# Identity fills between two phases: twelve copies moved from VectorE to GpSimd, behind a zero fill that now comes first

## The chip, the cores and the metric

The kernel runs on one core of one Trainium2 chip. A core has five engines that run their own queues of instructions and meet through semaphores: TensorE (PE in the profile, with its weight loads as PEld), VectorE (DVE), ScalarE (ACT), GpSimd (POOL) and SyncE (SP), whose queue issues the DMAs. The metric is the device time of one execution in microseconds (us); lower is better.

## The reference

One layer of a bidirectional mixer. 128 context tokens and 2048 latent tokens of width 1024 are normalised, modulated and projected; half the channels (8 heads of 64) go through an RWKV-7 recurrence in both directions, the other half through a gated short convolution, and both through one output projection.

```python
def step(S, inp):                       # per direction and head, S is 64 x 64
    r_t, w_t, k_t, v_t, kk_t, a_t = inp
    s_kk = einsum('bdhij,bdhj->bdhi', S, kk_t)
    S = S * w_t[..., None, :] - s_kk[..., :, None] * (kk_t * a_t)[..., None, :] \
        + v_t[..., :, None] * k_t[..., None, :]
    return S, einsum('bdhij,bdhj->bdhi', S, r_t)
...
y = ys[:, 0] + flip(ys[:, 1])           # both directions
y = groupnorm(y) * gn_w + gn_b + bonus * v
ya = y * silu(g_a)
yb = b_gate * short_conv(c_gate * u_conv) * silu(g_b)
out = x + gate * (concat(ya, yb) @ w_out)      # then a last RMS norm
```

Outputs are the new context and latent tokens and the final context states.

## The kernel before

The program has three phases. Phase 1 projects blocks of 384 tokens on TensorE with fp32 split in two halves (lines 182 to 184), prepares the recurrence's operands and spills them to device memory. Phase 2 runs the recurrence in chunks of 64 tokens: 17 stages, each with eight units in either direction. Phase 3 is the output projection and the last norm.

In phase 2 the recurrence within a chunk becomes linear algebra. For each stage the kernel forms masked products of the chunk's operands (`Gm`, `Fm`, evicted by VectorE at L1037 and by ScalarE at L1048 and L1051), inverts the 16 triangular 64x64 systems of the stage, and builds one 128x128 operator E for each unit, which then carries the state from chunk to chunk (L1220, L1246). The inverse goes through these steps, with the names used in the profile:

- VectorE gathers the diagonal blocks in `dg` (L1058), turns them into `ab` (L1063) and does a first elimination step (L1081, then L1082, which writes `ab` again). ScalarE begins the result `zt` (L1073 to L1075; L1075 reads `ab`).
- GpSimd runs the elimination in 15 rounds of three operations, `ztmp` (L1091) and twice `zt` (L1094).
- VectorE turns `zt` into `zr` and `zd` (L1102, L1105). ScalarE copies the diagonal parts from `zd` into the tile `zb` (L1111). TensorE and ScalarE fill the off-diagonal part: psU (L1119), copied at L1122, psW (L1127), evicted into `zb` at L1130.
- TensorE multiplies `zb` with F (psX, L1171); ScalarE writes the result into the stack `stf` (L1175).
- The operators are products of two stacks (psE, L1189), masked by VectorE (L1194).

A stack is a tile of 128 partitions by two blocks by 2 x 8 x 64 values, 8 KB a partition. `stf0` and `stf1` hold one factor for the two directions, `stg0` and `stg1` the other one in even stages, `sth0` and `sth1` in odd ones. In partitions 0 to 63 block 0 of every stack is eight identities beside each other, for each of two heads; that part is written once, by `presetS`. The other parts are filled in every stage by DMA (L956) and by ScalarE (L1160, L1161, L1175). `zb` is zeroed once by `zero` (L907) and keeps its zero quarter for all stages.

All of these tiles are made in `setup_rest`, which runs at the start of phase 2's main part, when phase 1 has given back its memory. The pools are stacks: `stf`, `stg`, `zb` and the small `zr`, `zd` lie in the pool `l1` one behind the other, over the memory of phase 1's activations (two tiles of 24 KB on that side). `sth` lies in a pool on the other side. A tile's first write waits for the last users of the phase 1 tiles under it.

The order of the queues: in the main part of phase 2 and in phase 3, TensorE, VectorE and ScalarE follow an order that is written out in the source (`SEQ`, `LATE`). GpSimd, the DMA queue and everything between the phases, `setup_rest` and the work of the first stages ahead of the written order, are ordered by the framework's planner, which lets each engine take what its model of the program says is ready. In a queue, an instruction that waits holds all behind it.

```python
i2b = lambda n: B.I2[:].unsqueeze(1).broadcast_to((128, n, 64))
...
SEQ: "... bu+1 Ev010 I+2 S20 ... ab+3 ... pre+3 ... zr+2 ... zd+2 ..."   # word+d: of the stage d ahead
```

The words I, ab, pre, zr are the steps above: in the body of stage s the inverse of stage s+2 starts and the `ab` of stage s+3 is made.

Of the kernel before, what the change touches and what calls it, by code (L numbers as in the profile page):

```python
# [6 lines left out]
F32 = mybir.dt.float32  # L7
# [808 lines left out]
def phase2(K):  # L816
    nc, tc, A, S = K.nc, K.tc, K.A, K.S
    V, G, P, T = nc.vector, nc.gpsimd, nc.scalar, nc.tensor
    D = nc.sync.dma_start
    MF, MG, ME = (0, 1), (0, 1), (2, 3)  # L820
    B = Ctx()
    O = Ctx()
# [27 lines left out]
    def new_slot(pool):  # L850
        i = len(B.slots)
        B.slots.append([tuple(pool.tile([128, 8, w], F32, tag=f"{n}{i}{d}", name=f"{n}{i}{d}", bufs=1) for n, w in (("F", 128), ("GA", 128), ("Q", 64))) for d in range(2)])
# [8 lines left out]
    def setup_rest():  # L861
        O.l0 = Pool(K, "p2l0", "left")
        O.l1 = Pool(K, "p2l1", "left")
        O.pS = Pool(K, "p2S", "left", 4, PSUM)
        O.p2 = Pool(K, "p2s", "left", 2, PSUM)
        O.r2 = Pool(K, "p2r2", "right")
        new_slot(O.r2)
        cp = O.l0
        vec = cp.tile([128, 4], F32, name="vec2")
        D(vec[:], A["vec"][:, V_GW:V_GW + 4])  # L870
        B.gwh = cp.tile([128, 4], F32, name="gwh")
        V.tensor_scalar(B.gwh[:], vec[:], 0.5, None, ALU.mult)
        B.geps = cp.tile([128, 1], F32, name="geps")
        V.memset(B.geps[:], 64e-5)
        B.pc = cp.tile([64, 2, 8, 34], F32, name="pc")
        for d in range(2):
            D(B.pc[:, d], S[f"pc{d}"].rearrange("(e c) n -> c e n", c=64))

        B.fs = ring(O.l1, 2, [128, 2, 2, 8, 64], "stf", presetS)
        B.gs = ring(O.l1, 2, [128, 2, 2, 8, 64], "stg", presetS)  # L880
        B.gs2 = ring(O.r2, 2, [128, 2, 2, 8, 64], "sth", presetS)
        B.zb = O.l1.tile([128, 16, 64], F32, name="zb")
        zero(B.zb)

    def ring(pool, n, shape, name, init=None):
        l = [pool.tile(shape, F32, name=f"{name}{i}") for i in range(n)]
        if init:
            for t_ in l:
                init(t_)

        def get():
            l.append(l.pop(0))
            return l[-1]
        get.tiles = l
        return get
# [10 lines left out]
    def zero(t_):  # L906
        G.memset(t_[:], 0.0)  # L907
# [5 lines left out]

    def presetS(t_):
        for hd in range(2):
            V.tensor_copy(t_[0:64, 0, hd], B.I2[0:64].unsqueeze(1).broadcast_to((64, 8, 64)))

    def tl(shape, tag, b, pool=None, dt=F32):
        return (pool or O.l0).tile(shape, dt, tag=tag, name=f"{tag}_{K.u()}", bufs=b)
# [465 lines left out]

    def main():
        setup_rest()
        for b, n, t in order_of(range(-3, 0)):
            K.body = b
# [259 lines left out]
```

## Time and profile before

| | |
|---|---|
| median of 3 runs | 1586.96 us (1585.86 to 1587.49) |
| profiled execution, its time | 1585.76 us |
| its span, first to last instruction | 1583.9 us |
| mean granted TensorE clock | 0.982 |
| TensorE busy | 1501.7 us, 95% |
| VectorE busy | 1137.6 us, 72% |
| ScalarE busy | 770.6 us, 49% |
| GpSimd busy | 570.9 us, 36% |
| chain of waits by engine | PE 57%, POOL 18%, DVE 10%, issue 7%, DMA 5%, ACT 3% |

How to read it. Busy time is a share of the whole span, over stages with different limits; the chain of waits follows the work that ended last back from the end. In the chain, a line gives the start, the length and what ran. In a timeline of one engine a line gives the start, the time, the engine, source line and operation, output and input tiles with their shapes, the count of instructions merged into the line, and in brackets the idle time before it with what ended it. In a list of waits the numbers are the total, the times and the longest. In a list of stretches come the length, busy time and count of instructions of TensorE, its weight loads, VectorE, ScalarE and GpSimd, then the granted TensorE clock, the DMA engines' busy share and GB/s. In a list of groups, the busy time and the mean in ns of one stand behind the count.

The last projection of phase 1 ends near 948.8 us; the scan of phase 2 runs from there to about 1340 us, with parts of phase 3 mixed in towards its end.

### The profile page before, as it was taken

The page shows a single profiled execution, that of the slowest core. Times are in us where ns is not written, and L with a number is a line of the kernel's source. Part 1 is how long each engine was busy: PE and PEld are TensorE (multiplying, and loading weights), DVE is VectorE, ACT ScalarE, POOL GpSimd, SP SyncE. Part 2 cuts the span into 40 slices and gives each one's busy share as a digit, 9 for nine tenths or more (in the row PEclk, how much of TensorE's full clock was granted, in tenths as well). Part 3 has the DMA queues.
Part 4 walks back from the last instruction along what each step waited for, and adds up shares of the span by engine and source line. Part 5 has one row for each costly group of instructions (what it writes and reads, how often), then busy time and mean ns, then how long its engine had stood idle before and what let it go on. Part 6 is the DMA issues. An engine that isn't in the chain of part 4 may idle for free.

```text
span 1583.9 us, 39394 instructions
## 1 busy us (share of the span) xinstructions
PE 1501.7 (95%) x16208; PEld 1382.2 (87%) x16208; DVE 1137.6 (72%) x1960; ACT 770.6 (49%) x1460; POOL 570.9 (36%) x961
## 2 busy tenths in 40 slices
PE   5899999999999999999999998999999887899998
PEld 2799999999999999899999997888888776778786
DVE  5889996673999735349985438899898977746533
ACT  4466652432555213225551117887778767523221
POOL 0033331000333100013322705888888885212221
PEclk8899999999999999999999998999999999999999
DMA  9569999663878865447897537567576754645442
GB/s 371 197 168 269 269 268 335 216 222 112 218 231 227 203 230 181 145 137 209 262 242 271 184 125 193 151 177 195 167 205 167 186 149 149 186 134 188 147 144 93
DMA packets 204580, 313.78 MB, mean 198 GB/s; under 512 B 58089, under 2 KB 147561, under 8 KB 190321
## 3 DMA queue, kind: packets, MB, share of 16 engines
q1 hardware_dynamic: 168816, 311.13, 63.3%
q10 hardware_dynamic: 35584, 0.14, 1.4%
q8 instruction: 127, 2.08, 0.6%
q14 instruction: 53, 0.43, 0.1%
HBM read 208.05 MB, written 103.17 MB: 196 GB/s over the span
## 4 chain that ended last, share of the span: by engine, by line
PE 57%; POOL 18%; DVE 10%; issue 7%; DMA 5%; ACT 3%; SPq 1%; ACTq 0%; DVEq 0%; POOLq 0%
POOL zt L1094 11%; POOL ztmp L1091 7%; PE psu L1503 4%; PE psu L1505 4%; PE psu L1504 4%; PE mmb L182 2%; PE mmb L184 2%; PE mmb L183 2%; PE mmc L182 2%; PE mmc L184 2%; PE mmc L183 2%; PE mmu L184 2%; PE mmu L182 2%; PE mmgb L183 2%; PE mmgb L182 2%
## 5 line engine op out<-in xcount | busy, mean ns | idle before, releaser
L1094 POOL TENSOR_TENSOR zt<-zt,ztmp 128x30 f32<-128x30 f32 (+7 forms) x510 | 217.5, 426 | 39.8
L1091 POOL TENSOR_TENSOR ztmp<-ab,zt 128x60 f32<-128x60 f32 (+7 forms) x255 | 137.7, 540 | 65.3 <-DVE ab L1082 45.6
L410 POOL TENSOR_TENSOR sh<-rawl 128x384 f32<-128x384 f32 (+1 forms) x48 | 47.1, 997 | 210.4 <-ACT rawl L401 210.4
L1220 PEld LDWEIGHTS psS<-sv,E 128*64 128x64 f32 x2176 | 81.5, 137 | 40.7 <-DVE sv L1246 18.7
L1220 PE MATMUL psS<-sv,E 128*64 128x64 f32 x2176 | 102.4, 228 | 15.1 <-DVE sv L1246 10.4
L1194 DVE TENSOR_TENSOR E<-psE,msk 128x512 f32<-128x512 f32 x136 | 90.6, 682 | 20.7 <-PE psE L1189 19.8
L1568 POOL TENSOR_TENSOR z<-z,x 128x512 f32<-128x512 f32 x32 | 42.7, 1337 | 148.9 <-DVE z L1562 86.2
L1175 ACT ACTIVATE stf<-psX 64x512 f32<-64x512 f32 x136 | 80.3, 591 | 10.6 <-PE psX L1171 8.1
L434 POOL TENSOR_TENSOR hsl<-sq,hsh 128x384 fp32r<-128x384 f32 (+1 forms) x24 | 32.5, 1356 | 141.9 <-ACT hsh L429 141.9
L1246 DVE TENSOR_TENSOR sv<-psS,pc 64x128 f32<-64x128 f32 x254 | 62.3, 271 | 20.0 <-PE psS L1220 19.4
L182 PE MATMUL mmg<-h,w 128*128 128x384 f32 (+1 forms) x216 | 70.9, 328 | 0.0
L183 PE MATMUL mmg<-h,w 128*128 128x384 f32 (+1 forms) x216 | 70.8, 328 | 0.0
L184 PE MATMUL mmg<-h,w 128*128 128x384 f32 (+1 forms) x216 | 70.7, 327 | 0.0
L219 POOL TENSOR_TENSOR hslq<-ssq,hshq 128x384 fp32r<-128x384 f32 (+1 forms) x4 | 4.8, 1207 | 174.8 <-ACT hshq L218 110.3
L182 PE MATMUL mmv<-h,w 128*128 128x384 f32 (+1 forms) x192 | 63.9, 333 | 3.7 <-ACT lf L665 3.1
L182 PE MATMUL mmb<-h,w 128*128 128x384 f32 (+1 forms) x192 | 63.6, 331 | 3.8 <-DMA w<-scr_wsp 3.8
L184 PE MATMUL mmb<-h,w 128*128 128x384 f32 (+1 forms) x192 | 63.6, 331 | 0.0
L183 PE MATMUL mmb<-h,w 128*128 128x384 f32 (+1 forms) x192 | 63.3, 330 | 0.0
L184 PE MATMUL mmv<-h,w 128*128 128x384 f32 (+1 forms) x192 | 63.3, 330 | 0.0
L183 PE MATMUL mmv<-h,w 128*128 128x384 f32 (+1 forms) x192 | 63.2, 329 | 0.0
L182 PE MATMUL mmc<-h,w 128*128 128x384 f32 (+1 forms) x192 | 63.1, 329 | 0.0
L184 PE MATMUL mmc<-h,w 128*128 128x384 f32 (+1 forms) x192 | 62.9, 327 | 0.1
(311 smaller groups left out, 5018.2 us busy)
## 6 DMA issues: line engine op xcount, KB each, us to landing
w<-scr_wsp SPq DMA_DIRECT2D x68, 1024.0 KB, 6.5
scr_wsp<-w SPq DMA_DIRECT2D x34, 1024.0 KB, 6.4
rr<-scr_ops SPq DMA_DIRECT2D x32, 1024.0 KB, 6.4
scr_ops<-xs SPq DMA_DIRECT2D x160, 192.0 KB, 6.5
wr<-in_win SPq DMA_DIRECT2D x34, 512.0 KB, 6.6
x<-in_x SPq DMA_DIRECT2D x17, 512.0 KB, 3.8
wadas<-in_wada SPq DMA_DIRECT2D x8, 1024.0 KB, 13.9
sv<-scr_vt SPq DMA_DIRECT2D x32, 256.0 KB, 4.0
```

The source lines that it names most:

```text
L182: T.matmul(ps[:, :n], w[:, 0, k], hh[:, 0, k, :n], start=k == 0, stop=False)
L183: T.matmul(ps[:, :n], w[:, 0, k], hh[:, 1, k, :n], start=False, stop=False)
L184: T.matmul(ps[:, :n], w[:, 1, k], hh[:, 0, k, :n], start=False, stop=k == 7)
L1091: G.tensor_tensor(tv, ab[:, j:j + 2, j + 2:32].unsqueeze(1).broadcast_to((128, kn, 2, n)), zt[:, :kn, j:j + 2].unsqueeze(3).broadcast_to(( ...
L1094: G.tensor_tensor(zt[:, :kn, j + 2:32], zt[:, :kn, j + 2:32], tv[:, :, r], ALU.subtract)
L1175: P.activation(g.fs[64:128, :, hd, e::2], g.ps["X"][e][hr_].rearrange("p a (b t) -> p b a t", b=2), AF.Copy, scale=-1.0)
L1194: V.tensor_tensor(g.E[n][:, k:k + 2].rearrange("p a b c -> p (a b) c"), pe[:].rearrange("p a b c -> p (a b) c"), B.msk[:, ME[g.d]].unsquee ...
L1220: T.matmul(g.sp[i // 4][r, q, hd, :], g.E[n][:, k, hd, r], g.sv[:, u, hd, :], start=True, stop=True)
L1246: V.tensor_tensor(dst, g.sp[i // 4][0:64, q], B.pc[0:64, d, 2 * p:2 * p + 2, c:c + 1].broadcast_to((64, 2, 64)), ALU.mult)
L1503: T.matmul(ps[:], mh[:, n], hi[:, cs], start=start and n == 0, stop=False)
L1504: T.matmul(ps[:], mh[:, n], lo[:, cs], start=False, stop=False)
L1505: T.matmul(ps[:], ml[:, n], hi[:, cs], start=False, stop=stop and n == 3)
```

## The change

`zb` is allocated and zeroed ahead of the three rings of stacks, and the identities are copied by GpSimd (`G`) in place of VectorE (`V`). There are three rings of two stacks with two copies each: twelve copies of 64 x 512 values. `zb` thereby lies in front of the stacks in its pool and no longer behind them.

```diff
             D(B.pc[:, d], S[f"pc{d}"].rearrange("(e c) n -> c e n", c=64))
 
+        B.zb = O.l1.tile([128, 16, 64], F32, name="zb")
+        zero(B.zb)
         B.fs = ring(O.l1, 2, [128, 2, 2, 8, 64], "stf", presetS)
         B.gs = ring(O.l1, 2, [128, 2, 2, 8, 64], "stg", presetS)
         B.gs2 = ring(O.r2, 2, [128, 2, 2, 8, 64], "sth", presetS)
-        B.zb = O.l1.tile([128, 16, 64], F32, name="zb")
-        zero(B.zb)
...
     def presetS(t_):
         for hd in range(2):
-            V.tensor_copy(t_[0:64, 0, hd], B.I2[0:64].unsqueeze(1).broadcast_to((64, 8, 64)))
+            G.tensor_copy(t_[0:64, 0, hd], B.I2[0:64].unsqueeze(1).broadcast_to((64, 8, 64)))
```

## The prediction

> **What bounds the kernel now.** First the page's chain of waits, by line:
>
> ```profile
> POOL zt L1094 11%; POOL ztmp L1091 7%; PE psu L1503 4%; PE psu L1505 4%; PE psu L1504 4%; PE mmb L182 2%; PE mmb L184 2%; PE mmb L183 2%; PE mmc L182 2%; PE mmc L184 2%; PE mmc L183 2%; PE mmu L184 2%; PE mmu L182 2%; PE mmgb L183 2%; PE mmgb L182 2%
> ```
>
> GpSimd's inverse (L1091, L1094) is the costliest single thing on it. Next, who released GpSimd between 945 and 1345 us, how busy it is in one stage of the scan, and where its unbroken run ends:
>
> ```profile
> POOL ztmp L1091 <- DVE ab L1082: 16.5, 2, 14.5
> ...
> 964.00:988.00 24.00, 23.13 (x591) 20.39 (x584) 16.59 (x31) 16.88 (x33) 20.24 (x44) 0.95 0.61 170
> ...
> 1306.52 0.31 POOL L1091 TENSOR_TENSOR ztmp<-ab,zt 128x60 f32<-128x60 f32 x1
> ```
>
> GpSimd waited for VectorE's `ab` twice: 14.5 us before the first inverse of the scan, and once more for 2.0 at the very end (16.5 less 14.5). In between, inverses stand one behind the other, 20.24 of 24 us busy, the rest issue. Whatever moves the start of that first inverse therefore moves the whole scan. So I read the chain between the phases, on which the edit lies:
>
> ```profile
> 948.86 0.42 DVE bsv L590
> ...
> 950.04 1.07 DVE stf L916 x3
> 951.12 0.67 DVE stg L916 x2
> 951.78 0.40 DVE ov L619
> 952.18 0.67 DVE stg L916 x2
> 952.86 0.96 DVE zr L1102
> ...
> 953.96 1.23 PE psU L1119 x39
> 955.20 0.67 DVE sth L916 x2
> 955.87 2.39 DVE GA L1037 x4
> ...
> 959.91 2.08 DVE ab L1063
> 961.99 0.28 DVE F L1037
> 962.27 1.02 DVE dg L1081
> ...
> 963.48 0.76 DVE ab L1082
> ...
> 964.37 0.30 POOL ztmp L1091
> ```
>
> From the last projection to GpSimd's start, 948.86 to 964.37, the chain is VectorE almost alone, and the twelve copies of L916 stand in it. That is the part the change takes out.
>
> **The change, part by part.**
>
> *VectorE loses 12 copies.* From the end of `bsv` (949.28) to the first `stg` (951.12) is 1.84; `stg` twice 0.67; and the four `sth`:
>
> ```profile
> 954.49 1.38 DVE L916 COPY sth<-I 64x512 f32<-64x512 f32 x4
> ...
> 948.76 1.98 PE L1019 MATMUL psGm<-rr 64*64 64x128 f32 x64
> ```
>
> Together 1.84 + 1.34 + 1.38 = 4.55 us. `GA` could then start at 951.3; its products (psGm) are out at 950.74, so TensorE does not hold it. VectorE alone would give 4.55.
>
> *But ScalarE runs beside it, nearly without a gap*, and VectorE's next steps need it:
>
> ```profile
> 948.86 0.62 ACT L1160 COPY stg<-GA 64x512 f32<-64x512 f32 x1 [2.49 <-PE mmb L184]
> ...
> 952.72 0.61 ACT L1161 COPY stg<-Q 64x512 f32<-64x512 f32 x1
> 953.85 0.63 ACT L1073 ACTIVATE zt<-idt 128x512 f32<-128x512 f32 x1 [0.52 <-DVE gwh L872]
> ...
> 954.65 2.51 ACT L1111 COPY zb<-zd 32x512 f32<-32x512 f32 x4
> 957.19 0.62 ACT L1160 COPY sth<-GA 64x512 f32<-64x512 f32 x1
> ...
> 959.49 1.18 ACT L1122 COPY zd<-psU 32x512 f32<-32x512 f32 x2
> 960.70 0.65 ACT L1051 COPY F<-psFm 128x256 f32<-128x256 f32 x2
> 962.02 0.42 ACT L1075 ACTIVATE zt<-ab,ph 128x16 f32<-128x16 f32 x1 [0.68 <-DVE ab L1063]
> ```
>
> The brackets are all its idle time from 948.86 on: 0.52 (it waited for VectorE's first `zr`, now early) and 0.68 (for `ab`). If the planner keeps ScalarE's order, the copies of F (L1051) can start only 0.52 earlier, 960.18, and the first of the pair is out at about 960.50 (half of 0.65). VectorE's mask of F, which comes between the two `ab` steps and needs that copy, then starts about 960.55 where the chain has 961.99: 1.4 us earlier. The second copy ends at 960.83 and L1075 at 961.25, both ahead of the last `ab` step (963.48 less 1.4 = 962.1), so they add nothing. Of the 4.55 us, 1.4 reaches GpSimd's start and 3.1 turns into VectorE waiting for ScalarE. I take 1.4; the ends are 0.5 (all ScalarE work in front of the mask kept, and nothing beyond the 0.52) and 4.55.
>
> *GpSimd gets the memset first and then 12 copies*, ahead of the inverse on its queue; no DMA is moved, on any queue. A GpSimd copy of 64x512 is in no row. The nearest, and the copy on VectorE:
>
> ```profile
> L1568 POOL TENSOR_TENSOR z<-z,x 128x512 f32<-128x512 f32 x32 | 42.7, 1337 | 148.9 <-DVE z L1562 86.2 <-DVE z L1560 42.5 <-DMA mxa<-scr_mixT 12.7
> ...
> L434 POOL TENSOR_TENSOR hsl<-sq,hsh 128x384 fp32r<-128x384 f32 x20 | 28.4, 1421 | 122.5 <-ACT hsh L429 122.5
> ...
> L907 POOL MEMSET zb<- 128x1024 f32 x1 | 1.0, 952 | 40.8 <-PE mmb L184 40.8
> ...
> L916 DVE COPY stf<-I x4: 403/409/905, 949.2 to 950.7; 64x512 f32<-64x512 f32 x4
> ```
>
> Below: half of the memset, 0.48. Above: the two-input L434 scaled from 384 to 512, 1.89; the two-input L1568 at the very size 1.34. One input is nearer to the memset, so I take 0.65. The memset waited for the last product of phase 1, so it and all copies could start no earlier than 948.89 (its end 949.84): with 0.65 the last copy ends at 957.6, ahead of the 963.0 at which the inverse now wants the engine. In the code the zeroed tile moves from behind the four 8 KB stacks to their front, 32 KB lower, where a 24 KB activation tile of the block before lies; it may then be free about 12 us sooner, and the four `stf` copies with it. Either way the copies are hidden in the 14.5 us wait. That cover is gone at (963.0 - 949.84) / 12 = 1.10 us a copy; beyond it each 0.1 costs 1.2.
>
> *Who waits for the moved work.* ScalarE's L1111 needs the memset (954.65, at most 4 us earlier now): kept first on its queue, it is done by 949.84. The first reader of the stacks' identities is the operator product, which now waits for GpSimd instead of VectorE:
>
> ```profile
> 967.99 1.05 PE L1189 MATMUL psE<-stg,stf 128*64 128x128 f32 x12 [0.24 <-ACT stf L1175]
> ```
>
> Eight copies by 949.84 + 8 x 0.65 = 955.0; even at 1.34 they are in by 960.6. Costs nothing. While GpSimd's memset ran, VectorE's first copy took 905 ns instead of 409; the new copies can hold a VectorE step in the same way, some 0.5 each, but VectorE has 3.1 us to lose, so I cost that at nothing too.
>
> *Does 1.4 reach the end?* The second inverse of the scan needs its own `ab`:
>
> ```profile
> 987.17 0.69 DVE L1082 TENSOR_TENSOR ab<-ab,dg 128x512 f32<-128x512 f32 x1
> 988.40 0.29 POOL L1091 TENSOR_TENSOR ztmp<-ab,zt 128x60 f32<-128x60 f32 x1
> ```
>
> Ready 987.86, wanted 988.40: 0.5 us of room. For the other 0.9 the stage's TensorE and ScalarE work must come earlier as well; it hangs on the same ScalarE queue, which is 0.5 to 1.2 earlier, so I take it as passed on. After that GpSimd runs unbroken to 1306.5 and every later wait follows it.
>
> **The clock.** In the same gap TensorE stands still, and its granted clock (the third column from the right) falls:
>
> ```profile
> 953.96 1.92 PE L1119 MATMUL psU<-zr,GA 32*32 32x32 f32 x64 [3.23 <-DVE gwh L872]
> ...
> 957.00:960.00 3.00, 3.00 (x34) 2.67 (x32) 2.96 (x7) 2.94 (x6) 0.00 (x0) 0.50 0.97 221
> ...
> 966.00:969.00 3.00, 2.76 (x64) 2.12 (x56) 0.29 (x1) 2.20 (x4) 2.46 (x7) 0.92 1.05 386
> ```
>
> After 3.23 us of idling it works at 0.50 and is back at 0.92 only in 966 to 969. With `zr` 3.18 us earlier (1.84 + 0.67 + 0.67), psU could start at 950.78, right behind psGm, and this wait is all but gone. The Trainium skill, "TensorE: Matmul & The Clock Gate", Why this matters for your kernels, says to leave no gaps over some 3 us, as one idle window halves the clock; the trace agrees with 3.23 us. By that rule TensorE would keep full speed here, unless a longer wait opens behind it. In the sum the clock is worth nothing by itself, because ScalarE sets the time, and the 1.4 us stands with it or without it; it matters in rival D.
>
> **The rivals.**
> *A, more of it arrives.* The planner orders ScalarE anew, now that `ab` comes early, and puts the four `sth` copies (957.19 to 959.47, 2.28 us) behind L1075. ScalarE's limit falls by 2.28: 1.4 + 2.28 = 3.7 us, 1583.3 us; VectorE's own limit is 4.55. Against it: in the trace the planner had them ahead.
> *B, nothing arrives.* Stage 0 is as late as before, GpSimd waits for the second `ab`; only the 0.5 us of room is gained: 1586.5.
> *C, slower: GpSimd's copies are dear.* At 1.89 us each behind a memset that still ends at 949.84 they last until 972.5, 8.2 us later than the inverse now starts: 1595. It is slower at all from (964.37 - 949.84) / 12 = 1.21 us, and by 3.2 us from 1.48. For it: the inverse's small operations stretch beside VectorE's two-input steps. Against: a one-input copy, and much of VectorE's work there reads PSUM.
> *D, the slow clock moves.* TensorE runs dry after psU and the products behind it, since the copy L1122 on ScalarE comes no earlier than 959.0; the wait is then longer than the one removed, and the half clock reaches some 5 us into stage 0, where TensorE is busy 23.13 of 24 us. Half of 5 is 2.5 lost against 1.4 gained: 1588.1. It is slower than before from 2.8 us at half clock beyond 966.
>
> **How the numbers follow.** Forecast 1.4 us: 0.47. A 0.22, B 0.13, C 0.07, D 0.11. The profiled run took 1585.76, 1.2 below the median of 1586.96; it would become 1584.4, and the median 1585.6, which I predict. About 0.2%, 3.2 us, is what a measurement of this kernel tells from no change. Faster by more: most of A, 0.19. Slower by more: C and a third of D, 0.10. Within: 0.71. The range goes from VectorE's limit, 1586.96 - 4.55 = 1582.4, to a little over D, 1588.6; C's and D's tails, about 0.12, are left out.
>
> **What the profile after would show.** No L916 on VectorE, twelve copies on GpSimd after L907 of about 0.65 us, and the memset ahead of 948.9 if its tile is free sooner. ScalarE without its 0.52 and 0.68 gaps; VectorE with a new wait of about 3 us before the mask of F or before `GA`. GpSimd's first scan inverse 15.5 less 1.4, about 14.1 us after `bsv` starts, and the second 24 us later without idling. The wait of psU gone. Wrong if GpSimd's copies end later than the last `ab` step, if the inverse after the first has to wait, or if ScalarE's order between 948 and 963 is another.

## The result: slower, and the profile after

| | before | after |
|---|---|---|
| median of 5 runs each on one chip | 1585.86 us | 1596.98 us |
| ratio, 95% interval | | 1.0065 [1.0044, 1.0087] |
| the same, 12 runs on a second chip | 1584.77 us (34 runs) | 1590.73 us, 1.0027 [1.0006, 1.0047] |
| profiled execution, its time and span | 1585.76, 1583.9 us | 1597.65, 1595.9 us |
| GpSimd's first scan inverse, after the end of phase 1 | 15.5 us | 14.2 us |
| the second | 39.6 us | 46.2 us |

By the two ratios the change costs 4 to 10 us where 1.4 us of gain was forecast. "End of phase 1" is here and below the end of the last product `mmb` in the same trace: 948.83 us before, 949.61 after. Phase 1 ends at 943.8 to 954.0 us in the traces here, so points in time are compared from there.

The timeline of GpSimd after the change (start, length, engine, line, operation, tiles; idle time before it in brackets):

```profile
938.17 0.95 POOL L907 MEMSET zb<- 128x1024 f32 x1 [29.25 <-PE mmb L184]
939.06 2.46 POOL L916 COPY stf<-I 64x512 f32<-64x512 f32 x4
949.67 2.53 POOL L916 COPY stg<-I 64x512 f32<-64x512 f32 x4 [8.15 <-PE mmb L184]
952.15 2.27 POOL L916 COPY sth<-I 64x512 f32<-64x512 f32 x4
963.81 0.28 POOL L1091 TENSOR_TENSOR ztmp<-ab,zt 128x60 f32<-128x60 f32 x1 [9.38 <-DVE ab L1082]
...
985.45 0.60 POOL L1094 TENSOR_TENSOR zt<-zt,ztmp 128x30 f32<-128x30 f32 x2
...
995.79 0.29 POOL L1091 TENSOR_TENSOR ztmp<-ab,zt 128x60 f32<-128x60 f32 x1 [9.74 <-DVE ab L1082]
```

All of the new work is where the prediction put it, and the first inverse is 1.3 us earlier against the end of phase 1. Then GpSimd stands still for 9.74 us in front of the second inverse, where it had no such wait before. The waits of GpSimd from 945 to 1345 us say the same (total, times, longest; before it was 16.5, 2, 14.5):

```profile
POOL ztmp L1091 <- DVE ab L1082: 21.1, 3, 9.7
```

The third of these waits, 2.0 us long, is the one at the very end that stood there before. From the second inverse on GpSimd again runs without a break, so the delay stays in this trace: the scan's last inverse ends 8.2 us later than before, 7.4 of it counted from the end of phase 1. The other 3.8 us of the span came after it and were not followed up.

The second inverse waits for its `ab`, at the end of a long chain through the first stage of the scan, most of it on TensorE. TensorE before, then after the change:

```profile
956.52 2.89 PE L1019 MATMUL psFm<-rr 64*64 64x128 f32 x32 [0.64 <-DVE GA L1037]
959.34 1.97 PE L1028 MATMUL psQm<-idt,rr 128*128 128x128 f32 x8
...
969.59 1.40 PE L1119 MATMUL psU<-zr,GA 32*32 32x32 f32 x62
```

```profile
951.23 1.20 PE L1119 MATMUL psU<-zr,GA 32*32 32x32 f32 x64 [0.17 <-DVE zr L1102]
...
954.39 1.25 PE L1028 MATMUL psQm<-idt,rr 128*128 128x128 f32 x8 [1.16 <-DVE GA L1037]
956.84 1.69 PE L1019 MATMUL psFm<-rr 64*64 64x128 f32 x32 [1.19 <-DVE GA L1037]
960.25 2.89 PE L1019 MATMUL psFm<-rr 64*64 64x128 f32 x32 [1.72 <-ACT Q L1048]
...
964.78 1.73 PE L1119 MATMUL psU<-zr,GA 32*32 32x32 f32 x56
966.44 4.16 PE L1171 MATMUL psX<-F,zb 64*64 64x128 f32 x58
970.94 0.70 PE L1171 MATMUL psX<-F,zb 64*64 64x128 f32 x6 [0.34 <-issue]
```

Three things are new. The one wait of 3.23 us is gone, and three of 1.2 to 1.7 us stand in its place. The second stage's U (`psU`, 964.78), which stood behind X (`psX`) and the first E product (`psE`) before (969.59), now stands ahead of X. And Q (`psQm`) stands ahead of F (`psFm`). Nothing of this is in the edit: the planner orders everything between the phases, and it ordered anew. The granted clock (third column from the right) in stretches of 3.41 us:

```profile
958.74:962.15 3.41, 1.91 (x26) 1.91 (x28) 2.41 (x2) 3.31 (x8) 0.00 (x0) 0.50 1.08 207
962.15:965.57 3.42, 3.42 (x114) 3.09 (x110) 2.56 (x6) 1.89 (x6) 1.44 (x5) 0.50 1.05 222
...
979.22:982.64 3.42, 3.42 (x42) 3.42 (x42) 2.57 (x5) 0.91 (x2) 2.95 (x7) 0.50 0.00 0
982.64:986.05 3.41, 3.41 (x70) 3.41 (x69) 2.35 (x5) 0.00 (x0) 2.79 (x9) 1.00 0.02 5
```

Half clock lasts here from 958.74 to 982.64, seven such stretches, through most of the scan's first stage; before it was 952.84 to 966.48, four stretches. The DMA queue of SyncE changed as well. Before, then after:

```profile
948.86 1.22 SPq L956 DMA_DIRECT2D stg<-scr_ops  x2
952.21 0.32 SPq L621 DMA_DIRECT2D scr_mixT<-ov  x1
```

```profile
951.76 0.32 SPq L621 DMA_DIRECT2D scr_mixT<-ov  x1
952.18 1.23 SPq L956 DMA_DIRECT2D stg<-scr_ops  x2
```

A store that must wait for VectorE's `ov` now stands ahead of the scan's first loads, so all of them start 3.3 us later on the clock, 2.5 us later after phase 1.

So there were three suspects: the clock (T1 in the expectations), the order on TensorE (T2) and the transfers (T4). A fourth was to be excluded: GpSimd's work itself (T3).

### The profile page after: what moved, and what is told of

Same layout as the page of the kernel before. It is cut to its first block, busy times and chain, and to the rows that moved or that the text cites. A ratio compares the mean times of both kernels' runs of the same rounds, so it can differ in the third digit from the quotient of the medians.

```text
span 1595.9 us, 39400 instructions
## 1 busy us (share of the span) xinstructions
PE 1510.5 (95%) x16208; PEld 1389.4 (87%) x16208; DVE 1135.4 (71%) x1948; ACT 770.3 (48%) x1460; POOL 577.4 (36%) x973
## 4 chain that ended last, share of the span: by engine, by line
PE 58%; DVE 12%; POOL 10%; DMA 8%; issue 6%; ACT 4%; SPq 1%; ACTq 1%; DVEq 0%; POOLq 0%
POOL zt L1094 6%; PE psE L1189 4%; POOL ztmp L1091 4%; PE psu L1503 4%; PE psu L1504 4%; PE psu L1505 4%; PE mmb L182 2%; PE mmb L184 2%; PE mmb L183 2%; DMA w<-scr_wsp 2%; PE psS L1220 2%; PE mmc L182 2%; PE mmc L184 2%; PE mmc L183 2%; PE mmu L184 2%
## 5 line engine op out<-in xcount | busy, mean ns | idle before, releaser
L1094 POOL TENSOR_TENSOR zt<-zt,ztmp 128x30 f32<-128x30 f32 (+7 forms) x510 | 216.1, 424 | 39.8
L1091 POOL TENSOR_TENSOR ztmp<-ab,zt 128x60 f32<-128x60 f32 (+7 forms) x255 | 138.0, 541 | 69.8 <-DVE ab L1082 50.1
L1220 PEld LDWEIGHTS psS<-sv,E 128*64 128x64 f32 x2176 | 82.9, 138 | 39.3 <-DVE sv L1246 19.7
L1194 DVE TENSOR_TENSOR E<-psE,msk 128x512 f32<-128x512 f32 x136 | 90.7, 683 | 25.2 <-PE psE L1189 24.2
L1568 POOL TENSOR_TENSOR z<-z,x 128x512 f32<-128x512 f32 x32 | 42.7, 1337 | 151.2 <-DVE z L1562 98.5
L1175 ACT ACTIVATE stf<-psX 64x512 f32<-64x512 f32 x136 | 80.3, 591 | 14.2 <-PE psX L1171 11.8
L1246 DVE TENSOR_TENSOR sv<-psS,pc 64x128 f32<-64x128 f32 x254 | 62.6, 273 | 23.0 <-PE psS L1220 22.4
L182 PE MATMUL mmb<-h,w 128*128 128x384 f32 (+1 forms) x192 | 62.8, 327 | 3.2 <-DMA w<-scr_wsp 3.2
L184 PE MATMUL mmk<-h,w 128*128 128x384 f32 (+1 forms) x184 | 60.3, 328 | 2.7 <-DVE w L154 2.7
L184 PE MATMUL mmu<-h,w 128*128 128x384 f32 (+1 forms) x192 | 62.8, 327 | 0.0
## 6 DMA issues: line engine op xcount, KB each, us to landing
wadas<-in_wada SPq DMA_DIRECT2D x8, 1024.0 KB, 13.7
```

Of the source, the lines that this page charges most:

```text
L182: T.matmul(ps[:, :n], w[:, 0, k], hh[:, 0, k, :n], start=k == 0, stop=False)
L184: T.matmul(ps[:, :n], w[:, 1, k], hh[:, 0, k, :n], start=False, stop=k == 7)
L1091: G.tensor_tensor(tv, ab[:, j:j + 2, j + 2:32].unsqueeze(1).broadcast_to((128, kn, 2, n)), zt[:, :kn, j:j + 2].unsqueeze(3).broadcast_to(( ...
L1094: G.tensor_tensor(zt[:, :kn, j + 2:32], zt[:, :kn, j + 2:32], tv[:, :, r], ALU.subtract)
L1175: P.activation(g.fs[64:128, :, hd, e::2], g.ps["X"][e][hr_].rearrange("p a (b t) -> p b a t", b=2), AF.Copy, scale=-1.0)
L1194: V.tensor_tensor(g.E[n][:, k:k + 2].rearrange("p a b c -> p (a b) c"), pe[:].rearrange("p a b c -> p (a b) c"), B.msk[:, ME[g.d]].unsquee ...
```

## The experiments

Every kernel but the first row of `after` (5 runs) ran 11 or 12 times beside the kernel before (34 or 35 runs) on the same chip; the rows come from several chips, so two kernels are best compared through their ratios to before. Single executions spread over 9 to 17 us, so a ratio is known to 0.15 to 0.2% only. The place of the second inverse in the one trace of each shows more, but it is a single execution: the changed kernel itself gave 46.2 and 42.7 us. Inverses are in us after the end of phase 1. "Steps" are stretches of 3.4 us at half clock within 35 us after phase 1. "Early U" means the second stage's U ahead of X.

| kernel | first inverse | second inverse | steps | early U | ratio to before |
|---|---|---|---|---|---|
| before | 15.5 | 39.6 | 4 | no | 1 |
| after | 14.2 | 46.2 | 7 | yes | 1.0065 [1.0044, 1.0087] |
| after_again | 14.2 | 42.7 | 4 | yes | 1.0027 [1.0006, 1.0047] |
| e1_zb_first | 15.1 | 39.0 | 3 | no | 0.9983 [0.9970, 0.9997] |
| e1_again | 15.1 | 39.1 | 3 | no | 1.0014 [1.0000, 1.0028] |
| e2_copies_only | 12.8 | 45.5 | 2 + 3 | yes | 1.0032 [1.0017, 1.0048] |
| e3_dve_dummies | 18.0 | 42.1 | 3 | no | 1.0012 [0.9997, 1.0028] |
| e4_order_b | 13.6 | 39.8 | 4 | no | 1.0008 [0.9993, 1.0023] |
| e5_order_a | 12.5 | 45.5 | 8 | yes | 1.0019 [1.0004, 1.0033] |
| e6_order_a_fill | 12.6 | 44.5 | 3 | yes | 1.0040 [1.0018, 1.0062] |
| e7_order_b_fill | 13.6 | 42.0 | 2 | no | 1.0014 [0.9998, 1.0030] |
| e8_lean_loads | 13.6 | 39.5 | 2 | no | 1.0008 [0.9994, 1.0022] |
| e9_before_lean | 15.8 | 40.2 | 2 + 1 | no | 1.0026 [1.0006, 1.0047] |
| e10_lean_fill | 13.6 | 41.1 | 1 | no | 1.0023 [1.0004, 1.0042] |
| e11_before_order_a | 15.4 | 43.4 | 5 | yes | 1.0032 [1.0013, 1.0051] |
| e12_a_late_u | 12.5 | 41.1 | 4 | no | 1.0008 [0.9990, 1.0025] |
| e13_b_early_u | 13.6 | 43.3 | 1 + 5 | yes | 1.0005 [0.9987, 1.0023] |
| e14_act_queue | 14.9 | 39.3 | 4 | no | 0.9990 [0.9973, 1.0007] |

### The two halves, and a late VectorE

e1 undoes the second half of the edit (`V.tensor_copy` again in `presetS`), e2 the first (zeroing last again). e3 keeps both and gives VectorE twelve copies of the same shape beside GpSimd's:

```diff
     def presetS(t_):
+        B.st = getattr(B, "st", []) + [t_]
+        free = B.st[len(B.st) % 2] if len(B.st) in (3, 4) else t_
         for hd in range(2):
+            V.tensor_copy(free[64:128, 0, hd], B.I2[64:128].unsqueeze(1).broadcast_to((64, 8, 64)))
             G.tensor_copy(t_[0:64, 0, hd], ...)
```

> Only the first half of the change: the inverse's tile is zeroed first, the identities are still filled in by VectorE. VectorE, TensorE, ScalarE and SyncE keep the order of the kernel before. Theory T1 (the clock: an early VectorE turns TensorE's one long wait between the phases into several short ones, and the half clock then lasts through the scan's first stage): no change, 1586 us, half clock from about 953 to 966. Theory T2 (the planner's new order of the instructions between the phases delays the first stage, the clock aside): no change, 1586. Theory T3 (GpSimd's own new work, the zeroing or the copies, costs the time): up to 1597 if it is the zeroing, 1586 if it is the copies.

> The zeroing moved first, the identities on VectorE, once more on another chip: the first run of it came out at 0.9983 of before [0.997, 0.9997], though no engine's order differs. If that was real: 0.998 again, 1582. If it was the spread of the first phase and of the half-clock steps: 1.000 within 0.15%, 1585.

> Only the other half: GpSimd fills the identities in, the zeroing stands last in the program as before. VectorE is as early as in the changed kernel, and TensorE's order is nearly its order. T1, T2 and T3 (copies) all say slower by about 0.7%, 1597 us, with the first masked E tile at about 973 to 974 and the second scan inverse on GpSimd at about 996; T3 (zeroing) says 1586.

> The whole change, and beside it VectorE still writes 12 tiles of the same shape (into partitions 64 to 127 of the stacks, which are overwritten later), so that it is as late as before and the order between the phases is that of the kernel before. GpSimd does all its new work. T1 and T2: no change against before, 1586 us (1584 to 1588), half clock from about 953 to 966 only, second scan inverse at about 988. T3: as the changed kernel, 1597.

The zeroing alone does nothing that holds: 0.9983 on one chip and 1.0014 on another lie on either side of 1, and the second inverse stays at 39.0 and 39.1 us. The gain of the first run did not come again. The copies alone bring the loss: 45.5 us and 1.0032. e2 is no clean half, though: TensorE also waited 3.57 us for GpSimd in it. With VectorE as busy as before and GpSimd doing all its new work (e3), TensorE keeps the old order and the ratio interval holds 1. Its second inverse, 42.1 us, is 2.5 later than before, not the same as expected; the first is as much later, since VectorE's and GpSimd's copies now ran beside each other and VectorE's first four took 0.68 us each instead of 0.40. So GpSimd's work by itself (T3) does not bring the loss; it comes only when VectorE is free early and the planner reorders.

### The order

In e4 the words between the phases are written out by hand, as the scan's are, and follow the order of the kernel before; e5 follows the order of the changed kernel:

```diff
-        for b, n, t in order_of(range(-3, 0)):
-            K.body = b
-            do(n, t)
         order = tc.manual_schedule(engines={mybir.EngineType.PE, mybir.EngineType.DVE, mybir.EngineType.Activation})
         order.__enter__()
+        K.body = -1
+        for word in BETWEEN.split():
+            n, t = word.split("@")
+            do(n, int(t))
...
```

```
e4: ... Gm0@2 U@0 ... Fm0@2 Qm1@2 Qm0@2 W@0 ... Fm1@2 X0@0 ... X1@0 ... E000@0 ... U@1 Gm0@3 E001@0 ...
e5: ... Gm0@2 U@0 ... Qm1@2 Qm0@2 ... Fm0@2 ... Fm1@2 ... W@0 U@1 ... X0@0 ... X1@0 ... E000@0 ... Gm0@3 E001@0 ...
```

Of the words only TensorE's are shown. Gm, Fm, Qm, U, W, X and E are its products psGm to psE, and the number behind @ is the stage, the first being 0. The new code moves the lines down by six or seven: L1097 below is L1091, L1088 is L1082. e5 leaves one thing of the planner's order out: there the third stage's G products also lie in between E products.

e11 is e5's order in the kernel before, without the change. e12 is e5 with only U@1 moved behind E000@0, e13 is e4 with only U@1 moved ahead of X0@0.

> The whole change, with the order of TensorE, VectorE and ScalarE between the phases written out by hand, as the kernel before has it (the products of state U of the first stage behind all G products of the third, F before Q, all of U of the second stage behind the first E). T2 (order alone): 1584 to 1586 us, since the early VectorE then only helps; the half clock has its 13 us as before or none. T1 (the short waits): 1592 to 1597, with half clock for 20 us and more into the first stage, since VectorE is as early as in the changed kernel and TensorE waits in small pieces.

> The whole change, with the three engines' order between the phases written by hand as the changed kernel's planner has it (Q before F, all of U of the second stage ahead of X of the first); only the interleaving of the second G product with the second E product is gone. T2 (TensorE's order): second scan inverse 43 to 46 us after the end of the first phase, 1592 to 1597 us. T1 (clock) says the same only if the half clock again has 17 us or more; with 14 or less it says 40 to 42 us and 1586 to 1589.

> The changed kernel once more, beside the others of this call. All theories: slower than before by 0.4 to 0.9%, 1593 to 1600 us, the second scan inverse about 46 us after the end of the first phase (39.6 before). T1 (the clock carries the loss) adds: half clock for 5 to 7 steps of 3.4 us between the phases, 17 to 24 us; before it was 10 to 14.

> The kernel before, without the change, with the hand-written order that the changed kernel's planner chose (Q before F, all of U of the second stage ahead of X of the first). If the order alone costs the time: second scan inverse 42 to 46 us after the first phase's end, 1588 to 1593 us. If the order only hurts with an early VectorE: 39.5 to 40.5 us, 1584 to 1586.

> The whole change with that same order, but U of the second stage put back behind the first E product; Q stays ahead of F. If the early U is what hurts in the order: second inverse 39 to 41 us with four half-clock steps or fewer, 1584 to 1588 us. If it is Q ahead of F: 42 to 46 us, six steps or more, 1588 to 1593.

> The whole change with the hand-written order of the kernel before, but all of U of the second stage ahead of X of the first. If the early U hurts: X starts 1 to 2 us later than the 14.7 us of that order, TensorE meets its late instructions inside X instead of inside U, second inverse 41.5 to 45 us against 39.8, 1588 to 1592. If not: 39.5 to 40.5, 1584 to 1587.

This is the clearest result. The seven traces with an early U have the second inverse at 42.7 us or later, all others at 42.1 or earlier; the means are 44.4 and 40.3. e11 has it at 43.4 us and 1.0032 without any of the change. GpSimd's wait in e11, in e12 and in e4 (it also grows with an earlier first inverse, so e12 waits longer than e11):

```profile
994.84 0.29 POOL L1097 TENSOR_TENSOR ztmp<-ab,zt 128x60 f32<-128x60 f32 x1 [5.38 <-DVE ab L1088]
```

```profile
992.28 0.29 POOL L1097 TENSOR_TENSOR ztmp<-ab,zt 128x60 f32<-128x60 f32 x1 [6.24 <-DVE ab L1088]
```

```profile
991.21 0.29 POOL L1097 TENSOR_TENSOR ztmp<-ab,zt 128x60 f32<-128x60 f32 x1 [3.92 <-DVE ab L1088]
```

From e5 to e12 the moved U takes 4.4 us off the second inverse; from e4 to e13 it adds 3.5. In both the number of half-clock steps moves with it. The rest of that order, Q ahead of F among it, costs 1.2 us (e12 against e4).

In whole runs the same shows only on the mean: the ratio is 1.0031 over the seven with an early U and 1.0009 over the ten others. Six of the seven have an interval above 1, but so have e9 and e10, which have no early U, and neither e5 against e12 (1.0019, 1.0008) nor e13 against e4 (1.0005, 1.0008) shows what the traces show. The scan carries part of the reason: its last inverse ends 388.6 to 396.3 us after phase 1 with an early U (mean 392.6) and 385.0 to 391.1 without (mean 388.6), so the delay reaches the end on the mean but not in every trace; e11's scan ends where that of before does, at 388.6 against 388.9. The whole-run times expected for after_again, e5 and e13 were too high by 1.7 to 3.4 us, and after_again was expected to have its second inverse near 46 us.

At equal steps (four each) after_again stands 2.9 us behind e4; from after_again to the first profile of the same kernel are 3.5 us more, with three more steps. With the 0.2 by which e4 stands behind before, this makes the 6.6 us. These are differences of single traces, and by themselves they do not show which part is the order and which the clock.

### The clock

Products without use in TensorE's waits, in e5's order (e6) and e4's (e7):

```diff
+            if word[0] == "Z":        # Z2 behind U@0, Z3 or Z4 behind Qm0@2, ...
...
+                for _ in range(int(word[1:])):
+                    T.matmul(B.fz[:], B.idt[:], B.msk[:].rearrange("p a b -> p (a b)"), start=True, stop=True)
+                continue
```

> The same order, with eight products without use of 128x512 put into TensorE's waits (two behind U, three behind Q, three behind the first F), so that it is busy from the end of the first phase to X. T1: the half clock goes, or falls to 7 us or less, and the second inverse comes at 39 to 41 us, 1584 to 1588. T2: second inverse stays at 43 us or more, though the clock is full, since U and the products stand where they stood.

> The whole change with the hand-written order of the kernel before (as in the run with that order above), and seven such products in TensorE's waits. T1: no half clock between the phases, first E mask 3 to 4 us earlier than the 19.8 us of that run, second inverse at 36 to 38 us (GpSimd then waits for nothing), 1581 to 1583. T4 (the transfers: the loads of the scan start 2 us and more later since a store stands ahead of them, and the third stage's rows land at 22 us whatever TensorE does): second inverse stays at 38.5 to 40 us, with a wait of TensorE for those rows, 1584 to 1587.

The clock stayed full until 19.6 us (e6) and 21.0 us (e7) after phase 1, and little or nothing was won: the second inverse came at 44.5 us where e5 had 45.5, and at 42.0 where e4 had 39.8, which neither expectation for e7 had. TensorE came to X and U earlier and stopped there, waiting for nothing that the list of waits shows ("issue"), and the half clock came with the stop. The stops of after, after_again, e4, e6, e7:

```profile
970.94 0.70 PE L1171 MATMUL psX<-F,zb 64*64 64x128 f32 x6 [0.34 <-issue]
```

```profile
969.81 0.44 PE L1171 MATMUL psX<-F,zb 64*64 64x128 f32 x6 [1.14 <-issue]
```

```profile
972.92 0.56 PE L1125 MATMUL psU<-zr,GA 32*32 32x32 f32 x23 [1.05 <-issue]
...
973.90 1.10 PE L1025 MATMUL psGm<-rr 64*64 64x128 f32 x32 [0.41 <-DMA rr<-scr_ops]
```

```profile
969.14 1.55 PE L1177 MATMUL psX<-F,zb 64*64 64x128 f32 x23 [4.50 <-issue]
```

```profile
969.31 1.22 PE L1125 MATMUL psU<-zr,GA 32*32 32x32 f32 x37 [3.07 <-issue]
```

Two readings. In time, these five stops end 21.3, 21.8, 21.5, 21.7 and 21.9 us after phase 1, however early TensorE arrives (e1 and e13 are the same, e3, e5, e11 and e12 come 22.4 to 24.3 us after it). In the program, they stand at the same instruction: after leaves 6 products of X behind the stop (e5, nearly the same order by hand, 7), and e6, which is e5 with 16 records of useless products ahead of it, leaves 23; e4 leaves 23 products of U, e7, with 14 such records, leaves 37.

The traces decide it. In the first 60 us after phase 1 the 18 traces have 40 such stops of TensorE of over 0.25 us, and counted in products from the end of phase 1 all of them stand at 259, 385 to 387, 512 or 513, 767, 893 to 895 or 1020 to 1022, so at a spacing of about 128 products (128 weight loads stand beside them). The list of DMA queues has a queue of the kind "instruction" whose count fits: 127 packets of 16 KB in the whole execution, in which TensorE has 16,208 products. The whole execution of before, and 966 to 968 us of e6 (packets, MB, share of the time of 16 DMA engines):

```profile
q8 instruction: 127, 2.08, 0.6%
```

```profile
q8 instruction: 1, 0.02, 3.5%
```

Each of the 40 stops ends 1.2 to 1.8 us after such a packet has ended; in e6 the packet ends 20.3 us after phase 1 and the stop 21.7. So TensorE waited for the next block of its own program, which came late on the full DMA engines. In the kernel before, the packet ends at 20.2 us and TensorE passes the place at 21.6 without a stop: it was just in time, and an earlier TensorE had nothing to win there (e1 comes earlier and stops for 0.70 and 0.27 us).

This also allows an estimate of what the clock costs behind that place. If half of the half-clock time between the end of the stop (or the passing of the place) and the second inverse is taken off, 17.2 to 19.1 us are left in all traces but e8 to e10, whose loads were moved, and after_again and e2 (20.9 and 20.7). The half taken off is 5.8 us in after, 4.9 in e5, 4.1 in e6, 3.3 in e13, 3.0 in e7 and 0.6 in e2, and nothing in the others of these. So by this estimate most of the loss of the first profile is the clock. after_again has none of it: there, as in e2, the third stage's first 32 G products stand in two groups of 16 that take 1.09 us each, where the 32 take 1.10 in e4. No run separates that from the rest of the order.

### The transfers

e8 has e4's order and puts the second stage's loads (stacks `sth`, rows of v) behind the third stage's rows `rr` on SyncE's queue, whose order it writes out by hand as well; e9 is the same in the kernel before; e10 is e8 with e7's useless products; e14 is e4 with the first two loads of `stg` on ScalarE's queue, so that the store no longer stands ahead of them:

```diff
-BETWEEN: ... gsL1@0 gsL0@0 svL0@0 svL1@0 fsL1@0 fsL0@0 ... gsL1@1 gsL0@1 ... L0@3 L1@3 ...
+BETWEEN: ... gsL1@0 gsL0@0 fsL1@0 fsL0@0 svL0@0 svL1@0 ... L0@3 L1@3 gsL1@1 gsL0@1 svL0@1 ...    # e8, e9, e10
...
-            D(t_[0:64, 1]..., src...)
+            (P.dma_start if k == 1 and g is sts[0].g[0] or k == 1 and g is sts[0].g[1] else D)(t_[0:64, 1]..., src...)    # e14
```

> The whole change, hand-written order of the kernel before on TensorE, VectorE and ScalarE, and on SyncE the loads that the second stage needs (its stacks, its rows of v: about 1 MB) behind the third stage's rows. T4 (the transfers hold TensorE: its own next instructions and the third stage's rows come through the same full DMA engines, and come at 21 to 22.5 us after the first phase's end): TensorE's wait inside the second stage's U (1.05 us in the run with that order) goes, the third stage's G products start at 18 to 20 us instead of 22.5, second scan inverse at 35 to 37 us (GpSimd without a wait, after a first one at 13.6), 1580 to 1583 us. T1 (clock) and T2 (order) without T4: no change against the run with that order, second inverse at 39 to 40 us, 1584 to 1587.

> The kernel before, VectorE filling the identities and the zeroing last, with the same orders and the same late loads as the run with the late loads. It asks what the change itself is worth once order and transfers are out of its way. If the early VectorE then reaches the end: first inverse at 15 to 15.5 us against 13.6, second at 36.5 to 38, 1582 to 1585 us, 1.5 to 2 us more than the run with the change. If it does not: the same second inverse in both, within 0.5 us.

> The run with the late loads, and beside it seven products without use in TensorE's waits, so that its clock stays full. T4 with the clock as the second cause: second inverse at 34.9 to 35.5 us, straight behind the first one, and no half clock before 20 us; 1579 to 1582. If TensorE's next instructions still come late, it waits inside U or X for them again, and the half clock follows that wait as it did in the other run with such products: second inverse 37 to 42, 1583 to 1588.

> The whole change with the hand-written order of the kernel before, and the first stage's first two loads issued on ScalarE's queue, so that no store stands ahead of them. T4: the transfers start at once after the first phase's end instead of 2.6 us later, TensorE's wait inside U (until 21.5 us) and the third stage's rows (22.5 us) come 1 to 2.5 us earlier, second inverse 37.6 (straight behind the first) to 38.8, 1582 to 1585 us. Without T4: 39.5 to 40 as with that order, 1585 to 1587.

The stops follow the transfers. With fewer loads ahead, the block of the program lands at 16.4 and 16.6 us after phase 1 in e8 and e10, the stop in U is gone, and the third stage's G masks start at 21.8 and 20.5 us instead of 23.7 (e4). But the next block, now behind the delayed loads, lands at 26.0 and 25.2, and the stop stands there (e8, then e10, its end 27.3 and 26.8 us after phase 1):

```profile
977.16 0.71 PE L1196 MATMUL psE<-stg,stf 128*64 128x128 f32 x9 [1.71 <-issue]
```

```profile
975.25 0.91 PE L1196 MATMUL psE<-stf,stg 128*64 128x128 f32 x6 [3.27 <-issue]
```

What was won goes back: 39.5 and 41.1 us. In e14 the loads start at once and no stop is left on the way to the second `ab` (one of 1.28 us ends at 38.9 us, beside it). Only the order of TensorE's work is left:

```profile
968.55 1.46 PE L1125 MATMUL psU<-zr,GA 32*32 32x32 f32 x64
969.95 1.10 PE L1025 MATMUL psGm<-rr 64*64 64x128 f32 x32
```

Yet its second inverse is at 39.3 us, not at 37.6 to 38.8: the half clock has its four steps there, and the store, which now landed later, held VectorE for 2.36 us in the middle of `GA`:

```profile
954.43 1.29 DVE L1043 TENSOR_TENSOR GA<-psGm,mkg 128x512 f32<-128x512 f32 x2 [2.36 <-DMA scr_mixT<-ov]
```

e14 is the best version of the whole change found, 0.9990 [0.9973, 1.0007], which is no measurable gain. e8 against e9 asks what the change is worth with order and loads equal: the first inverse is 2.2 us earlier, the second 0.7, which is neither of the two expectations. Their ratios overlap. e9, the kernel before with these orders by hand, is slower than before (1.0026) with a second inverse at 40.2 us, so not every loss in whole runs comes from the early U.

## Why the prediction was wrong, point by point

*VectorE loses 12 copies; ScalarE lets 1.4 through.* Right in size, first inverse 14.2 us after phase 1 against 15.5, but by luck. ScalarE's order did not stay, Q went ahead of F, and the copies of F started 12.3 us after phase 1, 0.4 later than before instead of 0.5 earlier. What made up for it is that VectorE's step L1081 now stood ahead of its mask of F instead of behind it:

```profile
960.07 1.12 DVE L1081 TENSOR_TENSOR dg<-ab 128x512 f32<-128x512 f32 x1
962.31 0.76 DVE L1037 TENSOR_TENSOR F<-psFm,msk 128x256 f32<-128x256 f32 x2 [1.12 <-ACT F L1051]
962.98 0.68 DVE L1082 TENSOR_TENSOR ab<-ab,dg 128x512 f32<-128x512 f32 x1
```

With other orders the whole change gave 12.5 to 14.9.

*GpSimd's copies.* Right: about 0.6 us each (2.46 / 4 and 2.53 / 4; 0.65 was taken), the memset 11 us sooner, the last copy out 9.4 us before the inverse. Rival C is out.

*"No DMA is moved, on any queue."* Wrong in effect. The edit moves none, but the planner put a store ahead of the loads.

*"Does 1.4 reach the end?"* This is the step that failed. It gave the second inverse 0.5 us of room and took the other 0.9 as passed on, because ScalarE's queue was earlier. `ab` of the second inverse hangs on TensorE: on its order, on its clock and on when the next block of its program and the third stage's rows land. Instead of 1.4 us earlier the second inverse came 6.6 us later, counted from the end of phase 1 (3.1 in after_again), and no run brought it more than 0.6 us below the 39.6 us of before, with first inverses from 12.5 to 18.0. Even the 0.5 us was partly an illusion. The first inverse's last steps in the trace of before, then after:

```profile
985.91 1.34 POOL L1091 TENSOR_TENSOR ztmp<-ab,zt 128x60 f32<-128x60 f32 x1
987.33 1.00 POOL L1094 TENSOR_TENSOR zt<-zt,ztmp 128x30 f32<-128x30 f32 x2
```

```profile
985.06 0.31 POOL L1091 TENSOR_TENSOR ztmp<-ab,zt 128x60 f32<-128x60 f32 x1
985.45 0.60 POOL L1094 TENSOR_TENSOR zt<-zt,ztmp 128x30 f32<-128x30 f32 x2
```

Before, the same steps took 1.4 us longer, while VectorE made the next `ab` (the 987.17 row of the prediction). Unstretched, GpSimd would have ended at 986.9, a microsecond ahead of `ab` (an estimate from these four rows): the row of inverses looked unbroken, but without the stretching its second one would have waited for `ab`.

*The clock, and rival D.* The wait of psU did go (0.17 us), but TensorE did not keep full speed: the clock fell after waits of 1.16 and 1.19 us. D comes nearest to what happened: the half clock moved into the first stage. Its way there was another, short waits for `GA` and Q and not one longer wait for L1122, and its term, 5 us beyond 966, was mis-sized: 16.6 us in the first profile. In after_again the half clock ends only 2.6 us later than in before, counted from phase 1, and that execution still loses 3.1 us at the second inverse. So D alone is not all of it; TensorE's new order and the late block of its program were in no rival. "If ScalarE's order is another" stood among the signs of error, but ScalarE's alone.

*A and B.* First inverses of 12.5 us show that A's earlier start is possible; they brought nothing. B (the second inverse as late as before, GpSimd waiting for it) is what the late-U versions of the whole change come nearest to, with the second inverse at 39.3 to 42.0 us; e3, with its busy VectorE, stands at 42.1 without a wait.

Open is why the planner chose the new order (that it reacts to an early VectorE is shown by e3, how is not), why the half clock takes four steps in one execution and seven in the next, and what in the order, beside the clock, makes after_again and e2 late.

## What to carry to other kernels

Where a planner orders the queues, an edit that frees one engine can change the order of all, DMA queue included; compare orders, not only durations, and price the new order before the freed time. A wait that heads a chain is worth only the room up to the next wait, and "no idle time" does not prove there is none: look whether the last instructions before it are stretched. Between two phases with full transfers, a shorter compute path may just arrive earlier at the same late data, or at the next block of an engine's own program.

## What was unexpected in the hardware

- The granted clock changes in steps of 3.41 us: half-clock spells of 3.4, 6.8, 10.2, 13.7, 17.1, 23.9 and 27.3 us. The Trainium skill, "TensorE: Matmul & The Clock Gate", What's actually happening, gives a free-running window of 3413 ns, and the traces agree. It also says that at least one busy window brings the full clock back and that all behind the first 3.4 us or so runs at it; here they differ, since TensorE worked through 3.42 of 3.42 us at 962.15 and stayed at 0.50 for five more windows. And the clock fell in after behind waits of 1.16 and 1.19 us, neither of them a window long; TensorE was busy for 2.01 of the 3.41 us ahead of the fall.
- TensorE stopped up to 4.50 us in the middle of one tile's products, waiting for its own program. The stops stand about 128 products apart, or a multiple of that, each ends 1.2 to 1.8 us after a 16 KB instruction packet, and they moved by one block when the transfers were moved.
- GpSimd's small steps of 0.31 us took 1.34 us beside VectorE's two-input steps, and VectorE's 64x512 copy 0.68 us instead of 0.40 beside GpSimd's.
